# Result rows of a mixture of experts written by index past the empty slots, with another order of the last job, the eighth block's gates and the last block

## The chip, the cores and the metric

The kernel runs on one core of one Trainium2 chip, in float32. The metric is the device time of one execution, in microseconds (us). The program has five instruction streams: TensorE (PE in the rows, PEld for its weight loads), VectorE (DVE), ScalarE (ACT), GpSimd (POOL) and SyncE (SP). SP issues nearly all the loads, POOL the transfers by index. Sixteen DMA engines carry all transfers.

## The reference, cut to what matters

One encoder layer over 512 tokens of width 1024. The first part (a gated MLP group and a windowed attention group) gives `h`. Then comes the part that the change touches: 32 experts of width 256, of which each token uses two, and a gate of the embeddings `p`.

```python
def hier_moe(xt, ...):                 # top-1 of 4 groups, top-2 of its 8 experts
    ...
    for e in range(N_EXPERTS):
        hdn = jax.nn.silu(xt @ w_gate[e]) * (xt @ w_up[e])
        y = y + comb[:, e:e + 1] * (hdn @ w_down[e])
    return y

h = h + hier_moe(m, ...)
gate = jax.nn.sigmoid(h @ w_ple_gate[i] + b_ple_gate[i])
h = h + gate * rmsnorm(p[i] @ w_ple_proj[i], g_ple[i])
return rmsnorm(h, g_final)
```

## The kernel before, in words

**Front part, to about 200 us.** Projections, the gated MLP and the attention, with weights and inputs split into two parts of float32r (`mm3`), and the routing. Near 55 us the split of the queries ends (`V.tensor_tensor(qs...)`, the last operation on the way to the scores); near 82 us SP starts to load `w_out` (`s5a<-in_wo`, `s5c<-in_wo`), which ACT and DVE split (`load_parts`).

**Experts, about 190 to 471 us.** The two rows of each token (one per chosen expert) are sorted into slots. An expert among the first 20 places has 64 slots, a later one 32 (`LATE = 20`); a slot without a token holds an index beyond 511. `jobs` are 17 pairs of experts: ten with 2 x 64 slots, the others with 2 x 32, among them job 5 (`EXTRA`), which takes what overflows from places 7 and 8. Job `j` gathers its tokens from `h_dr` by index (`tokens_in`; an index beyond the bound moves nothing), transposes and scales them (`tokens_T`, `tokens_T2`), multiplies by the gate and up weights (`gate_up`), applies SiLU (`hidden`), transposes (`hidden_T`), multiplies by the down weights (`down`) and adds this to the scaled token rows (`base`, `scaled`) in one of two buffers `yo[j % 2]`. `rows_out(j)` then writes the whole buffer, empty slots too, to its rows of the DRAM tensor `y_dr` (1728 rows of 4 KB) with one plain DMA from POOL; jobs 15 and 16 stay on the chip. The weights of a pair of experts are 6 MB; SP loads them into seats as these come free, at most three loads in flight (`pace`).

**Blocks.** The 512 tokens are sorted by the job that ends their second row, and finished in nine blocks: 0 to 6 of 64 tokens, 7 and 8 of 32 (four column quarters side by side, `shape`, `chunk`). Block `b` gathers its tokens' two rows from `y_dr` (`f_in`, after job `FETCH[b]`), adds them (`f_add`), adds rows that have not gone through DRAM by a matmul with a 0/1 matrix (`f_sel`, `f_add2`), transposes (`f_T`, `f_T2`), multiplies by the 1024x1024 gate weights in eight steps `k` (`f_gate`), adds the bias, applies the sigmoid and the product with the `p` part (`f_post`), sums the squares (`total`), takes the root (`rstd`; for block 8 `ROOT` with ACT's square root) and writes out by index (`f_norm`, `f_out`).

**Order of the work.** `Plan` records every operation with its dependences, an estimated cost and a rank, and `issue` then sends them out greedily: the operation that could begin first by the estimate, then the lowest rank. So each engine's order is fixed when the program is built. `plan.gate` makes the recorded operations wait for others, `plan.behind` places them after others in the order, and `plan.fill` lets dummy matmuls into bank 7 (`filler`, line 361) fill gaps that the plan expects on TensorE. Nearly every instruction is recorded on line 238 or, for two or more matmuls issued together, line 169.

**The end.** In job 16 (the last) the order is: `f_sel`, `f_T` and `gate_up`, `hidden`, then `f_gate(7)` with all eight steps, `down`, `scaled` (the rows `own`), the fillers, the transposes of block 8 with `own`, `f_sel(8)`, `f_gate(8)`, its bias and sigmoid, and the last norm.

Of the kernel before, what the change touches and what calls it, by code (L numbers as in the profile page):

```python
# [4 lines left out]

# [31 lines left out]
WORK = (8, 9, 11, 12, 13, 14, 15)  # L37
SEL = (4, 12), (5, 13), (6, 14), (7, 15), (8, 15), (8, 16)
SETTLE = 5
P_AT = (6, 7, 8, 9, 10, 11, 12, 14)  # L40
SIZE = dict(a=2048, e=1024, b=2048, c=2048, d=1024, s1=6144,
            **{f"s{i}{h}": 2048 for i in (0, 2, 3, 4, 5, 6) for h in "acb"})
# [7 lines left out]
def f32(v):  # L50
    return v.bitcast(F32)
# [6 lines left out]
LOW7 = 0  # L58
# [27 lines left out]
class Plan:  # L86
# [45 lines left out]
    def note(self, e, method, call, args, kw):  # L132
        outs = [kw["out"] if "out" in kw else args[0]] + ([kw["accum_out"]] if "accum_out" in kw else [])
        ins = [getattr(a, "ap", a) if type(a) is bass.IndirectOffsetOnAxis else a
               for a in (*args[("out" not in kw):], *[v for k, v in kw.items() if k not in ("out", "accum_out")])]
        ins = [a for a in ins if isinstance(a, AP)]
        joins = e == "T" and bool(self.unit)
        i, after = self.unit[0] if joins else len(self.ops), set(self.gate)
        for a, writes in [(a, False) for a in ins] + [(a, True) for a in outs]:
            where = self.where(a)  # L140
            if where is None:
                continue
            place, box = where
            kept = []
            for j, b, w in self.mem.get(place, ()):
                hit = box[0] < b[1] and b[0] < box[1] and box[2] < b[3] and b[2] < box[3]

                if (hit and (w or writes) or b[4] != box[4]) and j != i:
                    after.add(j)
                covered = writes and box[0] <= b[0] and b[1] <= box[1] and box[2] <= b[2] and b[3] <= box[3]  # L150
                if not covered or j == i:
                    kept.append((j, b, w))
            self.mem[place] = kept + [(i, box, writes)]
            if e == "T" and writes:
                after.add(self.psum.get(place, i))
                self.psum[place] = i
        after.discard(i)
        first = outs[0]
        busy, late = self.cost(e, method, first, args, kw)
        size = 0  # L160
        if "dma_start" in method:
            first = next(a for a in (first, *ins) if a.space != bass.MemoryType.DRAM)
            size = 4 * first.free_size() * first.shape[0] / 360e3
        if joins:
            o = self.ops[i]
            first, last = (o[6], o[7], o[8]), (call, args, kw)
            o[1] += busy
            o[4] |= after
            o[6:10] = lambda: [c(*a, **k) for c, a, k in (first, last)], (), {}, (o[9] | self.behind) - o[4]  # L169
            return  # L170
        assert self.unit is None or e == "T"
        if self.unit is not None:
            self.unit.append(i)
        self.ops.append([e, busy, late, size, after, self.rank, call, args, kw, self.behind - after, self.fill, self.slack if e == "T" else 0.0])
# [82 lines left out]
def layer(ctx, tc, I, out):  # L257
# [5 lines left out]
    dr = ctx.enter_context(tc.tile_pool(name="dr", bufs=1, space=bass.MemoryType.DRAM))  # L263
    bank = [pp.tile([128, 512], F32, name=f"bank{i}") for i in range(8)]
    h_dr = dr.tile([512, 1024], F32, name="h_dr")
    y_dr = dr.tile([Y_ROWS, 1024], F32, name="y_dr")
    pace = dr.tile([128, 64], F32, name="pace")

    class Region:
# [44 lines left out]
    wr = pool.tile([128, 8, 36], F32, name="wr")  # L314
    tris = pool.tile([128, 128], BF, name="tris")
    oness = pool.tile([128, 128], BF, name="oness")
    small = pool.tile([128, 216], F32, name="small")
    gtmp = pool.tile([128, 512], F32, name="gtmp")
    idx = small[:, 0:17].bitcast(I32)
    fidx = small[:, 17:41].bitcast(I32)  # L320
    bad = small[:, 41:42].bitcast(I32)
    fst = small[:, 44:52]
# [33 lines left out]
        T.matmul(ps, lh, rl, start=False, stop=False)  # L356
        T.matmul(ps, ll, rh, start=False, stop=last)

    def filler(g):

        return lambda: nc.tensor.matmul(bank[g], oness, oness[:, None, :].to_broadcast([128, 4, 128]), start=True, stop=True)  # L361


    plan.on = True
# [108 lines left out]
    for g in range(4):  # L473
        q_ = q32[g % 2]
        V.scalar_tensor_tensor(q_, bank[g], 0.125, rbc, op0=OP.mult, op1=OP.mult)
        for v in range(2):
            p = slice(64 * v, 64 * v + 64)
            h = v * 4 + g
            S.activation(qs[h][p], q_[p], AF.Copy)
            V.tensor_tensor(qs[h][64 - 64 * v:128 - 64 * v], q_[p], f32(qs[h][p]), op=OP.subtract)  # L480


    f5, fe = Region("s5b"), Region("e")
# [470 lines left out]
    for p, o in sides:  # L954
        V.tensor_copy(WC[p, :, 0:3], bank[WB][p, 0:18].rearrange("p (a b c) -> p a b c", a=3, b=3, c=2)[:, :, :, o])


    plan.gate = set()
    by = [len(TILES[place[e]]) - 1 or 1 for e in range(FIRST)]
# [13 lines left out]
    def tables():  # L973
# [50 lines left out]
                    "p (a b c) -> p a b c", a=3, b=n // 2, c=2)[:, :, :, o])  # L1024

        take(256, n, slice(3, LATE // 2), sides)

        flat2 = lambda v: v.rearrange("p a b -> p (a b)")
        V.tensor_scalar(BX, P2, 6.5, None, op0=OP.is_gt)
# [12 lines left out]
        with plan.together():  # L1042
          for t in range(4):
            for i in range(2):
                T.matmul(bank[7][0:64, 320:320 + 4 * m], hq[:, 4 * i + t].rearrange("p a b -> p (a b)"),
                         RNQ[:, i, t].rearrange("p a b -> p (a b)"), start=t == 0 and i == 0, stop=t == 3 and i == 1)
        take(320, m, slice(LATE // 2, 17), ((slice(0, 32), 0), (slice(32, 64), 1)))
        V.tensor_copy(WC[64:128, :, LATE // 2:17], WC[0:64, :, LATE // 2:17])

        V.tensor_tensor(t3, P2[:, 0], P2[:, 1], op=OP.max)  # L1050
# [212 lines left out]

    def rows_out(j):
        r0, n = first_row(j), rows_of(j)[1].stop
        G.dma_start(y_dr[r0:r0 + n, :], yo[j % 2][:n])

    epsc = att_st[:, 28:29]

# [69 lines left out]
    def row(n, b):  # L1339
        return L[n + "q" if quarters(b) else n]  # L1340
# [4 lines left out]
    def f_in(b, n):  # L1345

        m = shape(b)[0]
        for i, v in enumerate((at("fy", b), at("fz", b))):
            G.memset(v, 0.0)
            ix = qidx[:, 2 * i + b - 5:2 * i + b - 4] if m == 4 else fidx[:, 8 * i + 8 + b:8 * i + 9 + b]  # L1350
            gather_rows(v, pieces(y_dr[0:n, :], m), ix, m * n - 1)

    def f_out(b):
        m = shape(b)[0]
# [41 lines left out]
    def rstd(b, i, g):  # L1396
        rsqrt(stat(b, i + 1), stat(b, 4), 1, -0.5 / 1024, stat(b, 5), bank[g][:, 500:501])
# [43 lines left out]
        S.activation(fT[:, 0:w // 2], bank[g][:, 0:w // 2], AF.Copy)  # L1441
        V.tensor_copy(fT[:, w // 2:w], bank[g][:, w // 2:w])

    def f_gate(b, g=3, cs=None):
        n, t, m = shape(b)
        cs = (0, m) if cs is None else cs
        for k in range(8):
            w = L["wg"][k // 2][:, k % 2]
            with plan.together():
                for q in range(n):  # L1450
                    T.matmul(bank[g][t * q:t * q + t, cs[0]:cs[1]], L["fT"][:, chunk(b, k)],
                             w[:, q * m + cs[0]:q * m + cs[1]], start=k == 0, stop=k == 7)

    def f_post(b, g=3, cs=None, o=2, root=False):
        c = slice(0, shape(b)[2]) if cs is None else slice(*cs)
        fx, fy, fple = at("fx", b)[:, c], at("fy", b)[:, c], at("fple", b)[:, c]
        V.tensor_tensor(fy, bank[g][:, c], row("bpl", b)[:, c], op=OP.add)
        S.activation(fy, fy, AF.Sigmoid)
        done = {len(plan.ops) - 1}
        V.tensor_tensor(fy, fy, fple, op=OP.mult)  # L1460
        V.tensor_tensor(fx, fx, fy, op=OP.add)
        if root and ROOT:

            plan.behind = done
            S.activation(stat(b, 7), epsc, AF.Sqrt)
            plan.behind = set()
            V.tensor_tensor_reduce(out=fy, in0=fx, in1=fx, scale=1.0, scalar=0.0, op0=OP.mult, op1=OP.add, accum_out=stat(b, o))
        else:
            S.activation(fy, fx, AF.Square, accum_out=stat(b, o))
# [9 lines left out]
    if True:  # L1479
# [15 lines left out]
        for j in range(nj):  # L1495
# [19 lines left out]
                plan.fill = filler(7) if j else None  # L1515
            load_after(j, 0)
            hidden(j)
            if norm is not None:
                plan.rank = R + LOW
                total(norm, 2, 7 if j < nj - 1 else 2)  # L1520
                plan.rank = R
# [19 lines left out]
                    f_add2(c, 4 if c > 6 else 3)  # L1541
            if j == nj - 1:
                plan.rank = R + LOW7
                f_gate(7)
                f_post(7)
                total(7, 2, 3)
                rstd(7, 2, 3)
                f_norm(7)
                f_out(7)
                plan.rank = R  # L1550
            if j + 1 < nj:
                base(j + 1)
# [9 lines left out]
            if b is not None:  # L1562
                f_T(b, FT[rows_of(j)[1].stop == 64])
                f_T2(b, FT[rows_of(j)[1].stop == 64])
            down(j, 1)
            scaled(j)
            if j < nj - 2:
                rows_out(j)
# [21 lines left out]
            for c in range(9):  # L1590
                if fetch[c] == j:
                    f_in(c, rows_n[c])

        fx, last = at("fx", 8), tokens_of(8, nj - 1)[:64]
        for i in range(2):
            T.matmul(bank[i][:, 0:128], fx[:, 128 * i:128 * i + 128], ident, start=True, stop=False, skip_group_check=True)
        for k in (0, 2, 1, 3, 4, 6, 5, 7):
            T.matmul(bank[k % 2][:, 32 * (k // 2):32 * (k // 2) + 32], own[:, 128 * k:128 * k + 128], last, start=False, stop=True,
                     skip_group_check=True)
        S.activation(L["fT"][:, 0:128], bank[0][:, 0:128], AF.Copy)  # L1600
        V.tensor_copy(L["fT"][:, 128:256], bank[1][:, 0:128])
        plan.rank += 1
        f_sel(8, [nj - 1], 4, src=own)
        f_add2(8, 4)
        plan.rank -= 1
        f_gate(8, 2)
        f_post(8, 2, root=True)
        total(8, 2, 3)
        if ROOT:
# [185 lines left out]
```

## Time and profile before

| what | value |
|---|---|
| median of 3 runs | 491.39 us (488.01, 491.39, 494.56) |
| the profiled execution: time, span of its trace | 489.91 us, 488.1 us |
| busy share of the span: PE, DVE, ACT, POOL | 95%, 62%, 35%, 20% |
| granted TensorE clock, mean | 0.984 |
| moved by DMA | 144.72 MB |

The span is the stretch that the trace covers; 1.81 us of the profiled execution lie outside it. Busy shares are means over stages with different limits. A clock of 1.00 means TensorE's full 2.4 GHz, 0.5 the lower level of 1.2 GHz. In a row of instructions the bracket says how long the engine sat idle before it and what ended that wait.

### The profile page before, as it was taken

How to read it: one execution, taken by the hardware profiler on the slowest of the kernel's cores; microseconds unless marked ns; L12 is line 12 of the kernel's file. 1: busy time of each engine (PE TensorE's matmuls, PEld its weight loads, DVE VectorE, ACT ScalarE, POOL GpSimd, SP SyncE). 2: the span in 40 equal slices, each digit the busy share in tenths (PEclk: the TensorE clock that was granted, in tenths of full speed). 3: DMA queues.
4: the chain of work that ended last, by engine and by line, in shares of the span. 5: the costliest groups of instructions: out<-in, count | busy, mean ns of one | idle time of the engine just before them, and what ended most of it. 6: DMA issues, size and time to landing. Idle time of an engine off the chain costs nothing.

```text
span 488.1 us, 8538 instructions
## 1 busy us (share of the span) xinstructions
PE 462.8 (95%) x2973; PEld 259.4 (53%) x2973; DVE 305.0 (62%) x991; ACT 172.7 (35%) x354; POOL 100.0 (20%) x131
## 2 busy tenths in 40 slices
PE   7999999999999998999999999799999898798994
PEld 4888887868678896543334333233343333333352
DVE  4985998899853566894435344426466665565553
ACT  4958576899913340100001001013212223213131
POOL 0000112313210002011541223312143233123001
PEclk9999999999999999999999999999999899799999
DMA  8874101356779986999988999999999999999801
GB/s 282 268 263 149 54 0 43 131 173 228 278 297 426 361 296 214 353 385 419 412 314 278 399 418 419 415 368 400 381 342 430 396 392 370 387 383 378 307 4 48
DMA packets 26590, 144.72 MB, mean 296 GB/s; under 512 B 4200, under 2 KB 4748, under 8 KB 14638
## 3 DMA queue, kind: packets, MB, share of 16 engines
q1 hardware_dynamic: 20190, 124.61, 67.3%
q0 software_dynamic: 6352, 19.51, 10.7%
q8 instruction: 25, 0.41, 0.3%
q14 instruction: 23, 0.19, 0.1%
HBM read 136.37 MB, written 10.77 MB: 301 GB/s over the span
## 4 chain that ended last, share of the span: by engine, by line
PE 82%; DMA 7%; DVE 6%; issue 2%; ACT 2%; SPq 0%; POOL 0%; POOLq 0%; ACTq 0%; DVEq 0%
PE bank L169 48%; PE bank L238 33%; DMA y_dr<-b 4%; DMA s3c<-y_dr,small 2%; DMA b<-in_xwq 1%; DVE b L238 1%; PE bank L361 1%; DVE c L238 1%; DVE s3a L238 1%; DVE small L238 1%; DVE s2c L238 1%; DVE e L238 0%; DVE s3c L238 0%; DVE s L238 0%; SPq L238 0%
## 5 line engine op out<-in xcount | busy, mean ns | idle before, releaser
L238 DVE TENSOR_SCALAR small<-small 128x1 f32<-128x1 f32 (+4 forms) x207 | 45.9, 223 | 4.3
L169 PE MATMUL bank<-s,c 128*32 128x256 f32 (+1 forms) x176 | 48.5, 491 | 0.0
L238 ACT ACTIVATE e<-bank,small 128x256 f32<-128x256 f32 (+1 forms) x17 | 8.0, 471 | 103.6 <-PE bank L169 103.6
L238 DVE SCALAR_TENSOR_TENSOR b<-bank,small,b 128x512 f32<-128x512 f32 (+1 forms) x32 | 24.0, 749 | 23.5 <-PE bank L169 23.3
L238 ACT ACT_TABLE_LOAD x20 | 25.7, 1283 | 9.8 <-PE bank L169 4.5
L238 DVE TENSOR_TENSOR c<-bank,cst 128x512 f32<-128x512 f32 (+1 forms) x34 | 18.6, 573 | 16.1 <-PE bank L169 15.4
L238 ACT ACTIVATE s3c<-s3c 128x512 f32<-128x512 f32 (+1 forms) x9 | 5.2, 582 | 64.7 <-DVE s3c L238 64.7
L238 ACT ACTIVATE s<-s,small 128x256 f32<-128x256 f32 (+1 forms) x48 | 25.5, 556 | 3.6 <-DVE small L238 3.6
L169 PE MATMUL bank<-s,e 128*64 128x512 f32 (+1 forms) x64 | 26.2, 626 | 0.0
L169 PE MATMUL bank<-s4b,e 128*64 128x512 f32 (+1 forms) x56 | 22.5, 630 | 2.7 <-DVE small L238 2.7
L238 POOL DMA_INDIRECT a<-h_dr,small x17 | 17.1, 1004 | 38.8 <-issue 12.0
L238 DVE SCALAR_TENSOR_TENSOR e<-bank,small,e 128x256 f32<-128x256 f32 (+1 forms) x17 | 8.2, 485 | 26.0 <-ACT e L238 24.4
L169 PE MATMUL bank<-s0a,c 128*32 128x256 f32 (+1 forms) x96 | 22.9, 454 | 0.4 <-DVE c L238 0.4
L169 PE MATMUL bank<-s5a,c 128*32 128x256 f32 (+1 forms) x96 | 22.9, 454 | 0.0
L238 DVE TENSOR_SCALAR b<-a,small 64x512 f32<-64x512 f32 (+2 forms) x23 | 14.4, 625 | 12.9 <-DMA y_dr<-b 9.9
L169 PE MATMUL bank<-s5b,e 128*64 128x512 f32 (+1 forms) x64 | 22.3, 597 | 0.0
L169 PE MATMUL bank<-s0b,e 128*64 128x512 f32 (+1 forms) x64 | 22.3, 596 | 0.0
L169 PE MATMUL bank<-s5c,c 128*32 128x256 f32 (+1 forms) x96 | 22.1, 451 | 0.0
L169 PE MATMUL bank<-s0c,c 128*32 128x256 f32 (+1 forms) x96 | 22.1, 451 | 0.0
L169 PE MATMUL bank<-s4a,c 128*32 128x256 f32 (+1 forms) x80 | 21.9, 498 | 0.0
L169 PE MATMUL bank<-s2a,s6c 128*64 128x512 f32 (+1 forms) x88 | 17.7, 560 | 4.1 <-ACT s6c L238 2.5
L238 POOL DMA_INDIRECT s3c<-y_dr,small x14 | 15.3, 1090 | 28.2 <-DMA y_dr<-b 25.7
(428 smaller groups left out, 1218.9 us busy)
## 6 DMA issues: line engine op xcount, KB each, us to landing
s<-in_wgu SPq DMA_DIRECT2D x7, 2048.0 KB
s0a<-in_wgu SPq DMA_DIRECT2D x7, 1024.0 KB
s0c<-in_wgu SPq DMA_DIRECT2D x7, 1024.0 KB
s0b<-in_wdn SPq DMA_DIRECT2D x7, 1024.0 KB
s5a<-in_wgu SPq DMA_DIRECT2D x7, 1024.0 KB
s<-in_wdn SPq DMA_DIRECT2D x7, 1024.0 KB
s5c<-in_wgu SPq DMA_DIRECT2D x7, 1024.0 KB
s4a<-in_wgu SPq DMA_DIRECT2D x7, 1024.0 KB
```

Source lines behind the costliest of these rows:

```text
L169: o[6:10] = lambda: [c(*a, **k) for c, a, k in (first, last)], (), {}, (o[9] | self.behind) - o[4]
L238: call(*args, **kw)
L361: return lambda: nc.tensor.matmul(bank[g], oness, oness[:, None, :].to_broadcast([128, 4, 128]), start=True, stop=True)
```

## The change

1. `y_dr` is a plain DRAM tensor with 17 views that are declared disjoint, one per job. Near the front part's 55 us, SP fills its 1728 rows from `x` with four DMAs from DRAM to DRAM, so that every row holds finite numbers.
2. `rows_for` computes on DVE a table `yidx` of destination rows, with 4096 added for an empty slot. `rows_out` writes by that index with a bound, so empty slots are passed over. The writes are declared independent of the gathers already recorded in `fetched`.
3. In the last job, only steps 0 to 4 of `f_gate(7)` stand ahead of `down`; steps 5 to 7 and the rest of block 7 (`f_post` to `f_out`) come behind it. ACT's sigmoid table is loaded by a dummy activation right after the SiLU.
4. For block 8, a matmul with the identity puts the bias into bank 2 ahead of the gates, four gate steps come before `f_sel(8)` and four after it, the sigmoid reads the bank directly, and at most nine fillers stand ahead of the last sum.

```diff
+AHEAD = 5
...
-    y_dr = dr.tile([Y_ROWS, 1024], F32, name="y_dr")
+    y_dr = nc.dram_tensor("y_dr", (Y_ROWS, 1024), F32).ap()
+
+    y_of = bass_types.dram_disjoint_views(y_dr, 17)
+    fetched = []
...
+    yidx = small[:, 216:233].bitcast(I32)
...
+    def filler(g, most=99):
+
+        left = [most]
+
+        def fill():
+            if left[0]:
+                left[0] -= 1
+                nc.tensor.matmul(bank[g], oness, oness[:, None, :].to_broadcast([128, 4, 128]), start=True, stop=True)
+
+        return fill
...
+    plan.gate = {len(plan.ops) - 1}
+    for i in range(0, Y_ROWS, 512):
+        n = min(512, Y_ROWS - i)
+        Y.dma_start(y_dr[i:i + n, :], I["x"][0:n, :])
+    plan.gate = set()
...
+    def rows_for(p, a, b, n, r0):
+
+        y = yidx[p, a:b]
+        V.tensor_scalar(y, idx[p, a:b], 511.5, 4096.0, op0=OP.is_gt, op1=OP.mult)
+        if b > a + 1:
+            V.scalar_tensor_tensor(y, iota32[p, 0:b - a], float(n), y, op0=OP.mult, op1=OP.add)
+        V.tensor_scalar(y, y, tokp1[p, 0:1], r0 - 1.0, op0=OP.add, op1=OP.add)
...
+    rows_for(slice(0, 128), 0, 3, 128, 64)
...
+        rows_for(slice(0, 128), 3, LATE // 2, 128, 64 + 384)
...
+        rows_for(slice(0, 64), LATE // 2, 16, 64, 64 + 64 * LATE)
+        rows_for(slice(0, 64), 16, 17, 64, 0)
...
-        G.dma_start(y_dr[r0:r0 + n, :], yo[j % 2][:n])
+        c = 16 if j == EXTRA else jobs[j][0] // 2
+        ix = bass.IndirectOffsetOnAxis(ap=yidx[:n, c:c + 1], axis=0)
+        plan.note("G", "indirect_dma_start", put, (), dict(out=y_dr[r0:r0 + n, :], out_offset=ix, in_=yo[j % 2][:n], in_offset=None,
+                                                           bounds_check=r0 + n - 1, oob_is_err=False, view=y_of[c]))
+
+    def put(out, view, **kw):
+
+        w = nc.gpsimd.indirect_dma_start(out=view, **kw)
+        for f in fetched:
+            tc.declare_no_dep(w.ins, f.ins, reason="other rows")
...
-    def f_gate(b, g=3, cs=None):
+    def f_gate(b, g=3, cs=None, ks=range(8), first=True):
...
-        V.tensor_tensor(fy, bank[g][:, c], row("bpl", b)[:, c], op=OP.add)
-        S.activation(fy, fy, AF.Sigmoid)
+        if root:
+
+            S.activation(fy, bank[g][:, c], AF.Sigmoid)
+        else:
+            V.tensor_tensor(fy, bank[g][:, c], row("bpl", b)[:, c], op=OP.add)
+            S.activation(fy, fy, AF.Sigmoid)
...
+            if j == nj - 1:
+
+                plan.behind = {len(plan.ops) - 2}
+                S.activation(stat(7, 7), epsc, AF.Sigmoid)
+                plan.behind = set()
...
-                f_gate(7)
-                f_post(7)
-                total(7, 2, 3)
-                rstd(7, 2, 3)
-                f_norm(7)
-                f_out(7)
+                f_gate(7, ks=range(AHEAD))
...
+        plan.behind = {plan.down}
+        plan.rank = R + LOW7
+        f_gate(7, ks=range(AHEAD, 8))
+        plan.behind = set()
+        f_post(7)
+        total(7, 2, 3)
+        rstd(7, 2, 3)
+        f_norm(7)
+        f_out(7)
...
+        plan.behind = {len(plan.ops) - 1}
+        with plan.together():
+            for q in range(4):
+                p = slice(32 * q, 32 * q + 32)
+                T.matmul(bank[2][p, 0:256], ident[:, p], row("bpl", 8), start=True, stop=False)
+        plan.behind = set()
...
-        plan.rank += 1
+        f_gate(8, 2, ks=range(4), first=False)
+        plan.behind = {len(plan.ops) - 1}
         f_sel(8, [nj - 1], 4, src=own)
+        plan.behind = set()
         f_add2(8, 4)
-        plan.rank -= 1
-        f_gate(8, 2)
+        f_gate(8, 2, ks=range(4, 8))
+        plan.fill = filler(7, 9)
```

## Rows read from the trace of the kernel before

**Rows 1.** Windows: busy us by engine (PE, PEld, DVE, ACT, POOL), granted clock, DMA share, GB/s.

```profile
300.00:320.00 20.00, 16.55 (x83) 6.65 (x84) 7.99 (x20) 2.27 (x6) 6.58 (x7) 0.91 1.01 409
400.00:420.00 20.00, 17.00 (x143) 6.32 (x142) 11.00 (x26) 5.40 (x8) 6.05 (x8) 1.00 0.99 383
```

**Rows 2.** Chain of waits that ended last: start us, us, what.

```profile
301.26 9.96 DMA y_dr<-b
...
395.90 8.46 DMA y_dr<-b
...
406.49 10.07 DMA s3c<-y_dr,small
```

**Rows 3.** Timeline around both stretches: who waited, and what ended the wait.

```profile
314.09 1.46 POOL L238 DMA_INDIRECT s3c<-y_dr,small  x1 [2.21 <-DMA y_dr<-b]
...
313.91 0.75 DVE L238 TENSOR_SCALAR b<-a,small 128x1024 f32<-128x1024 f32 x1 [2.70 <-issue]
...
315.05 1.00 PE L169 MATMUL bank<-s4b,e 128*64 128x512 f32 x1 [2.74 <-DVE small L238]
...
421.72 0.38 PE L169 MATMUL bank<-small,s3b 128*64 128x1 f32 x4 [1.87 <-ACT s3c L238]
```

**Rows 4.** Timeline: when job 14's seat s4a has landed, when TensorE uses it.

```profile
409.22 0.28 SPq L238 DMA_DIRECT2D pace<-s4a  x1
...
425.80 0.63 PE L169 MATMUL bank<-s4a,c 128*32 128x256 f32 x1
```

**Rows 5.** DMA: POOL's queue (packets, MB); issues, KB each, median us to landing.

```profile
q0 software_dynamic: 6352, 19.51, 10.7%
...
y_dr<-b POOLq DMA_DIRECT2D x10, 512.0 KB, 9.5
...
y_dr<-b POOLq DMA_DIRECT2D x5, 256.0 KB, 8.9
...
out<-s3c,small POOLq DMA_INDIRECT x9, 7.7
```

**Rows 6.** Tile y_dr: POOL's instructions, ns minimum, median, maximum.

```profile
L238 POOL DMA_DIRECT2D y_dr<-b x15: 567/597/730, 208.8 to 439.9; - x15
L238 POOL DMA_INDIRECT s3a<-y_dr,small x4: 998/1005/1020, 299.0 to 430.1; - x4
```

**Rows 7.** Windows of the front part and of full-rate loading, columns as before.

```profile
56.00:60.00 4.00, 4.00 (x22) 3.32 (x21) 3.97 (x15) 0.69 (x1) 0.62 (x1) 1.00 0.00 0
...
150.00:160.00 10.00, 10.00 (x60) 8.55 (x59) 4.13 (x18) 4.75 (x10) 0.17 (x1) 1.00 1.01 428
```

**Rows 8.** Timeline of the front part: end of query split, load, and its waiter.

```profile
54.92 0.69 DVE L238 TENSOR_TENSOR s0c<-s,s0c 64x512 fp32r<-64x512 f32 x1
...
82.53 0.80 SPq L238 DMA_DIRECT2D s5a<-in_wo  x2
...
86.44 0.73 ACT L238 ACTIVATE s4a<-s5a,cst 128x512 fp32r<-128x512 f32 x1 [3.87 <-DMA s5a<-in_wo]
```

**Rows 9.** Timeline: a small operation on slot tables.

```profile
210.24 0.16 DVE L238 TENSOR_SCALAR small<-bank 32x7 int32<-32x7 f32 x1
```

**Rows 10.** Timeline of the end: down, fillers, gates of block 8, its last sum.

```profile
469.14 0.59 PE L169 MATMUL bank<-s4b,e 128*32 128x512 f32 x1
...
471.19 0.82 PE L361 MATMUL bank<-oness 128*128 128x512 bf16 x3
...
477.31 1.05 PE L169 MATMUL bank<-s6b,s6c 128*32 128x256 f32 x16
478.29 3.19 PE L361 MATMUL bank<-oness 128*128 128x512 bf16 x14
478.42 0.42 DVE L238 TENSOR_TENSOR s3c<-bank,s3b 128x256 f32<-128x256 f32 x1 [1.02 <-PE bank L169]
...
480.60 0.08 DVE L238 DVE_READ_ACCUMULATOR2_ANT small<- 128x1 f32 x1
...
481.41 0.24 PE L169 MATMUL bank<-small,c 128*32 128x1 f32 x8
```

More of the change, by code (lines that the diff above doesn't have):

```diff
@@ L6 @@
 import concourse.bass as bass
+from concourse import bass_types
 import concourse.tile as tile
@@ L161, in note @@
         if "dma_start" in method:
-            first = next(a for a in (first, *ins) if a.space != bass.MemoryType.DRAM)
+            first = next((a for a in (first, *ins) if a.space != bass.MemoryType.DRAM), first)
             size = 4 * first.free_size() * first.shape[0] / 360e3
@@ L316, in layer @@
     oness = pool.tile([128, 128], BF, name="oness")
-    small = pool.tile([128, 216], F32, name="small")
+    small = pool.tile([128, 233], F32, name="small")
     gtmp = pool.tile([128, 512], F32, name="gtmp")
     idx = small[:, 0:17].bitcast(I32)
+    yidx = small[:, 216:233].bitcast(I32)
     fidx = small[:, 17:41].bitcast(I32)
@@ L357, in mm3 @@
         T.matmul(ps, ll, rh, start=False, stop=last)
-    def filler(g):
-        return lambda: nc.tensor.matmul(bank[g], oness, oness[:, None, :].to_broadcast([128, 4, 128]), start=True, stop=True)
+    def filler(g, most=99):
[5 more added lines that the diff above has]
+        return fill
     plan.on = True
@@ L955, in layer @@
         V.tensor_copy(WC[p, :, 0:3], bank[WB][p, 0:18].rearrange("p (a b c) -> p a b c", a=3, b=3, c=2)[:, :, :, o])
+    def rows_for(p, a, b, n, r0):
[4 more added lines that the diff above has]
+        V.tensor_scalar(y, y, tokp1[p, 0:1], r0 - 1.0, op0=OP.add, op1=OP.add)
+    plan.rank += 8
+    rows_for(slice(0, 128), 0, 3, 128, 64)
+    plan.rank -= 8
     plan.gate = set()
@@ L1351, in f_in, with kept @@
             gather_rows(v, pieces(y_dr[0:n, :], m), ix, m * n - 1)
+            if plan.on:
+                plan.ops[-1][6] = kept(plan.ops[-1][6])
+    def kept(call):
+        return lambda *args, **kw: fetched.append(call(*args, **kw))
     def f_out(b):
@@ L1442, in f_T2 @@
         V.tensor_copy(fT[:, w // 2:w], bank[g][:, w // 2:w])
-    def f_gate(b, g=3, cs=None):
+    def f_gate(b, g=3, cs=None, ks=range(8), first=True):
         n, t, m = shape(b)
         cs = (0, m) if cs is None else cs
-        for k in range(8):
+        for k in ks:
             w = L["wg"][k // 2][:, k % 2]
@@ L1451, in f_gate @@
                     T.matmul(bank[g][t * q:t * q + t, cs[0]:cs[1]], L["fT"][:, chunk(b, k)],
-                             w[:, q * m + cs[0]:q * m + cs[1]], start=k == 0, stop=k == 7)
+                             w[:, q * m + cs[0]:q * m + cs[1]], start=first and k == 0, stop=k == 7)
     def f_post(b, g=3, cs=None, o=2, root=False):
@@ L1565, in layer @@
             down(j, 1)
+            plan.down = len(plan.ops) - 1
             scaled(j)
@@ L1592, in layer @@
                     f_in(c, rows_n[c])
+        plan.behind = {plan.down}
[7 more added lines that the diff above has]
+        f_out(7)
+        plan.rank = R
         fx, last = at("fx", 8), tokens_of(8, nj - 1)[:64]
```

## Prediction

> **What bounds the kernel now.** I read the windows first. TensorE is busy 95% of the span; in the stage of the experts most windows of 20 us show it busy for 18 to 20 us, and the two worst are those of [rows 1], where it does 16.55 and 17.00 of 20. The DMA engines are full there too (1.01 and 0.99), so the second question is which of the two leads. [Rows 4] answer it: the load of s4a for job 14 has landed by 409.22, when SP's paced transfer behind it could go, and TensorE first reads it at 425.80. Weights are some 16 us ahead there; bytes alone do not hold TensorE up. What does hold it up stands in the chain of waits: between long runs of matmuls it goes through three transfers of `y_dr` [rows 2]. Around 301 us job 7's write is issued; DVE's `base` of job 9 must wait for it (it refills the same `yo`), and POOL's gather of block 1 too, so both begin only at about 314; TensorE, which needs a DVE copy queued behind that `base`, has sat idle 2.74 us by 315.05 [rows 3]. Its next matmuls then run long: 1.00 us in place of the 0.59 us that the same shape takes at [rows 10], first row, and the window's granted clock is 0.91. Around 396 us job 12's write takes 8.46 us, block 5's gather behind it 10.07 us, and TensorE waits 1.87 us for an activation fed by that sum [rows 2, 3]. So what a `y_dr` write is worth is read from these two holes. The third place is the end: after the last gates nothing overlaps, and each step removed is a step gained [rows 10].
>
> **The change part by part.** The sum is made against the profiled execution (489.91 us, of which 488.1 are span). That execution is 1.48 us below the median of the three runs, 491.39.
>
> *Smaller writes.* POOL's queue moved 19.51 MB [rows 5]. Of this the `y_dr` writes are 10 x 512 KB and 5 x 256 KB, 6.55 MB. Two loads of 1 MB, the 512 output rows of 4 KB and the 512 rows of `p` of 1 KB are 4.72 MB by the code. The remaining 8.24 MB must be the token gathers (1024 rows, 4.19 MB) and the gathers from `y_dr`: 4.05 MB, some 989 filled rows of 1600 written. The change therefore saves about 2.5 MB. At the 383 to 409 GB/s of [rows 1] that is 6 us of DMA time, but since the weights are ahead of TensorE I count none of it as such.
>
> What counts is when a write lands. Plain writes take 9.5 us at 512 KB and 8.9 at 256 KB, and output writes by index, also 256 KB, 7.7 [rows 5]. Size matters little, then: 0.6 us for half the bytes. If the small jobs were full, the ten large ones would hold 669 of 1280 rows, about 268 KB each, so a large write should land 0.6 us earlier by its size and up to 1.8 earlier by the row of output writes. A small write keeps most of its rows and gains 0 to 1.2. Against this, an instruction by index holds POOL 1.0 us in place of 0.6 [rows 6]; 0.4 us times 15 lies beside other work, except in front of a gather that has waited for this very write. The write also reads `yidx`, computed by DVE before its job's matmuls, so it adds no later wait. What is late next, if a write lands sooner, is the gather (10.07 us) or the matmul before the copy. I take 1.1 us in the first hole and 0.4 in the second: -1.5. Bounds: 0, and both holes gone with their slow clock, 2.74 + 1.87 us of waiting plus about 2.8 us of matmuls at half speed behind them, -7.4. The 2.8 is an estimate: eight matmuls, in pairs, 0.41 us too long in the first hole make 1.6 (1.00 against 0.59), and I add 1.2 for the second, where a matmul of the 256-column shape shows 0.63 [rows 4].
>
> *The fill.* 1728 rows of 4 KB are 7.08 MB, read and written in DRAM. SP may issue it when the last query split ends, 54.92 + 0.69 = 55.61 us [rows 8]. The DMA engines are idle from then (0.00 in [rows 7]) until `w_out` is loaded at 82.53; on SP nothing else is queued between, so no other issue waits. The cover is 26.9 us long, and it suffices from 263 GB/s up. No row shows a transfer from DRAM to DRAM. The nearest is loading at full rate, 428 GB/s [rows 7]: done by 72.2, cost 0. If each byte costs the engines twice, once in and once out, the rate is 214 GB/s and the end 88.7; `w_out`, first in line for ACT, which already waits 3.87 us for it [rows 8], would come up to 6.2 us later. ACT and then TensorE would shift by perhaps 4 of these, as ACT has little idle time behind that point. The bounds are 0 and +4; a gain is excluded, since nothing is removed. Neither row is near enough to decide, so I take +1.5.
>
> *Tables.* `rows_for` adds 11 small DVE operations by the four calls. At 0.16 us [rows 9] that is 1.8 us of DVE if none overlapped, in a stretch where TensorE does nearly 20 of 20 us. I take +0.3, bounds 0 and +1.8.
>
> *The last job.* Three steps of `f_gate(7)` move from before `down` to behind it. There the rows now show 0.82 us of fillers (471.19), while ACT and DVE scale `own` [rows 10]. A step of block 7 is half of a 16-record row, at most 0.53 us; three cover the scaling. TensorE's real work is the same, the fillers go: -0.8, if `hidden_T`'s copy is ready early enough for `down` to move up from 469.14; otherwise fillers return in front of it and the gain is 0. `f_post(7)` to `f_out(7)` come later by about 2 us; DVE and ACT have room for them while block 8's gates run, and their output write is issued before block 8's. If that cover failed, one DVE operation of 0.42 us would stand in block 8's way.
>
> *Block 8.* The bias matmul costs TensorE one more step, +0.5, partly in a wait for the copies of `fT`. DVE's bias addition goes: 0.42 us and a handover of 0.04 [rows 10], -0.46. The 14 fillers from 478.29 end after 481.4, while the sum of squares that the next matmul needs is read out at 480.68; nine fillers take 9/14 x 3.19 = 2.05 us and no longer delay it: -0.7. The table load moved up hides behind the matmuls. Together -0.7, and with the last job -1.5; bounds +0.5 and -2.
>
> **The sum.** -1.5 (writes) + 1.5 (fill) + 0.3 (tables) - 1.5 (end) = -1.2 us: 488.7 for an execution like the profiled one, 490.2 at the median. A measurement of this kernel can tell about 2% from no change, some 10 us. I forecast 490, no change that can be told.
>
> **The rivals.** *The fill collides.* At 214 GB/s the sum becomes -1.5 + 4 + 0.3 - 1.5 = +1.3, 492.7 at the median; it decides from 263 GB/s down, and grows by the full delay below that: at 180 GB/s the fill ends at 94.9, 12 us past the load, and the kernel is some 7 us slower (499). For it: reading and writing share the same engines and memory. Against it: the engines have an empty stretch, and their share measures how full they are, not how often a byte passes. The Trainium skill, "DMA: Bandwidth & Descriptors", section "Latency and other measured facts", lists copies between HBM tensors at 207 to 214 GB/s per direction, even at a good pitch; by it, as an estimate, the fill ends near 90 us and this rival holds. No run here shows such a copy yet.
>
> *The writes land early enough.* Both holes close and the clock stays up: -7.4 + 0.5 + 0.3 - 1.5 = -8.1, 483.3, with a little more if other waits for writes go too (DVE and POOL each wait for more of them). For it: in both holes the wait ends exactly with the write. Against it: landing depends little on size.
>
> *Passing over slots shortens nothing.* A transfer is over when its fullest engine is; empty slots stand together at the end of each 64, so some engines may simply go idle. Then 0 + 1.5 + 0.3 - 1.5 + up to 0.4 per write in the chain: +1.1, 492.5.
>
> **How the numbers follow.** Forecast 0.45; the fill collides 0.25, of which 0.08 at the low rates that cost over 2%; writes early enough 0.18, of which half with more than 2%; nothing shortened 0.12. That makes faster by over 2% 0.10, within 2% 0.82, slower 0.08. The range holds 8 in 10: from 482, the case of the early writes with a little more, to 497, between a collision at 214 and one at 180 GB/s.
>
> **What would show it.** The fill: DMA share between 56 and 92 us, and whether ACT's wait at s5a<-in_wo grows beyond 3.87 us. The writes: their landing, DVE's `base` and the gathers behind job 7 and job 12, and TensorE's busy time and clock in the windows of [rows 1]. The end: fillers gone behind `down`, and from the end of block 8's gates to its last sum some 2 us in place of 3. I am wrong if the order that the plan gives out changes elsewhere, since new operations shift every later choice, or if a gather now waits for more writes than it needs.

## The result: slower by 1.2%, and the profile after

The changed kernel takes 496.91 us (median of 6 runs, 494.11 to 501.07) where the kernel before, on the same chip, takes 490.94 (488.01 to 494.56). The ratio is 1.0124, 95% interval 1.0085 to 1.0162: 6.1 us more, 4.2 to 8.0. The forecast was 1.2 us less. Ratios here and below are made on one chip and leave disturbed runs out, so they are not always the quotient of two medians. The profiled execution after has a span of 495.2 us.

I look for the loss in the windows first. Here are windows of the kernel after (us; busy time of PE, PEld, DVE, ACT, POOL; clock, DMA share, GB/s):

```profile
300.00:320.00 20.00, 18.79 (x104) 7.16 (x101) 10.10 (x28) 3.22 (x7) 7.02 (x7) 1.00 0.99 393
320.00:340.00 20.00, 15.73 (x81) 5.49 (x77) 6.28 (x11) 3.51 (x6) 4.93 (x5) 0.99 1.00 388
340.00:360.00 20.00, 20.00 (x86) 6.98 (x88) 9.56 (x27) 2.99 (x5) 4.58 (x5) 0.84 1.00 370
...
400.00:420.00 20.00, 18.77 (x152) 7.15 (x156) 13.07 (x37) 5.08 (x8) 7.48 (x10) 0.91 1.01 403
```

At these times the holes of [rows 1] have filled up: 16.55 became 18.79 and 17.00 became 18.77. (The work there comes 8 to 12 us later than before: job 7's write is issued at 308.98 and no longer at 301.26, job 12's at 408.38 and no longer at 395.90.) But a new hole stands between 320 and 340, with a lower granted clock after it. What VectorE waits for, and what TensorE waits for from it, tells more (us in total, times, longest us). First before, then after:

```profile
DVE b L238 <- DMA y_dr<-b: 9.9, 7, 3.3
...
PE bank L169 <- DVE e L238: 0.3, 1, 0.3
```

```profile
DVE b L240 <- DMA y_dr<-b,small: 32.8, 11, 6.3
...
PE bank L171 <- DVE e L240: 9.0, 9, 3.8
```

`base`, the scaling that refills `yo`, now waits three times as long for the result writes, and TensorE waits 9.0 us in place of 0.3 for `e`, the tile of `hidden` and `hidden_T`. The timeline of after shows what this does at one of the 11 places (start us, us, instruction, idle time before it):

```profile
334.20 0.69 DVE L240 TENSOR_TENSOR s3a<-s3a,s3c 128x512 f32<-128x512 f32 x1
338.80 0.75 DVE L240 TENSOR_SCALAR b<-a,small 128x1024 f32<-128x1024 f32 x1 [3.91 <-DMA y_dr<-b,small]
339.47 0.48 DVE L240 SCALAR_TENSOR_TENSOR e<-bank,small,e 128x256 f32<-128x256 f32 x1
...
340.00 0.69 PE L171 MATMUL bank<-cst,e 128*128 128x128 f32 x2 [3.77 <-DVE e L240]
...
344.73 1.06 PE L171 MATMUL bank<-s0b,e 128*64 128x512 f32 x1
```

VectorE runs its instructions in the order of the plan. It stands 3.91 us at `base`, and the product of `hidden`, queued behind it, begins only when `base` is done. TensorE needs that product for `hidden_T` and idles 3.77 us, and a `down` matmul a little later takes 1.06 us in place of 0.59; the clock of the window from 340 to 360 is 0.84. The same step before:

```profile
332.07 0.74 DVE L238 TENSOR_SCALAR b<-a,small 128x1024 f32<-128x1024 f32 x1
...
335.51 0.47 DVE L238 SCALAR_TENSOR_TENSOR e<-bank,small,e 128x256 f32<-128x256 f32 x1
...
336.04 0.44 PE L169 MATMUL bank<-cst,e 128*128 128x128 f32 x2 [0.88 <-DVE small L238]
...
338.17 0.59 PE L169 MATMUL bank<-s0b,e 128*64 128x512 f32 x1
```

There the wait for the write is over when VectorE comes to `base`. The chain of waits after has the same picture once more, at job 11's write:

```profile
388.82 9.98 DMA y_dr<-b,small
398.82 0.48 DVE b L240
399.33 0.50 DVE e L240
399.88 6.68 PE bank L171 x30
```

Are the writes themselves slow? POOL's instructions of `y_dr` after (ns minimum/median/maximum), then landing of all transfers of `y_dr`, then the queue and the medians to landing:

```profile
L1307 POOL DMA_INDIRECT y_dr<-b,small x15: 935/1022/1527, 210.3 to 442.0; - x15
...
DMA to landing us min/median/max: 3.4/8.1/12.6
```

```profile
q0 software_dynamic: 6352, 17.00, 9.4%
...
y_dr<-b,small POOLq DMA_INDIRECT x15, 9.1
```

The queue moves 2.51 MB less than in [rows 5], as worked out. A write lands in 9.1 us, where 9.5 and 8.9 stood. So little was gained by passing over slots, but nothing that explains 6 us was lost either.

**Where the new order comes from.** `Plan` gives every DMA a transfer time from the bytes of the first operand that isn't in DRAM:

```python
first = next((a for a in (first, *ins) if a.space != bass.MemoryType.DRAM), first)
size = 4 * first.free_size() * first.shape[0] / 360e3
```

For the plain write that operand is `yo`: 1.46 us for 512 KB, 0.73 for 256 KB. For the write by index the change lists `out_offset` ahead of `in_`, so the first operand outside DRAM is the column of 128 offsets: 0.5 KB, 0.0014 us. The plan now holds the write for done 1.46 us sooner, finds that `base` can begin sooner, and sends it out ahead of work that TensorE needs. That is theory 1. The rivals: the writes themselves (theory 2); the new end; the fill and the tables.

### The profile page after: what moved, and what is told of

Read it like the earlier page. It is cut to its first block, busy times and chain, and to the rows that moved or that the text cites. A ratio compares the mean times of both kernels' runs of the same rounds, so it can differ in the third digit from the quotient of the medians.

```text
span 495.2 us, 8565 instructions
## 1 busy us (share of the span) xinstructions
PE 465.5 (94%) x2973; PEld 259.4 (52%) x2973; DVE 304.0 (61%) x1001; ACT 173.1 (35%) x355; POOL 106.9 (22%) x131
## 5 line engine op out<-in xcount | busy, mean ns | idle before, releaser
L240 DVE TENSOR_SCALAR small<-small 128x1 f32<-128x1 f32 (+5 forms) x211 | 46.3, 222 | 4.2
L171 PE MATMUL bank<-s,c 128*32 128x256 f32 (+1 forms) x176 | 47.2, 479 | 0.0
L240 DVE TENSOR_SCALAR b<-a,small 64x512 f32<-64x512 f32 (+2 forms) x23 | 14.0, 610 | 33.2 <-DMA y_dr<-b,small 32.8
L171 PE MATMUL bank<-s0b,e 128*64 128x512 f32 (+1 forms) x64 | 24.6, 662 | 0.2 <-DVE e L240 0.2
L171 PE MATMUL bank<-s5b,e 128*64 128x512 f32 (+1 forms) x64 | 24.7, 663 | 0.0
L171 PE MATMUL bank<-s,e 128*64 128x512 f32 (+1 forms) x64 | 24.5, 598 | 0.0
L1307 POOL DMA_INDIRECT y_dr<-b,small x15 | 15.5, 1037 | 40.8 <-DVE b L240 18.0
L171 PE MATMUL bank<-s0c,c 128*32 128x256 f32 (+1 forms) x96 | 23.7, 469 | 0.0
L171 PE MATMUL bank<-s5c,c 128*32 128x256 f32 (+1 forms) x96 | 23.7, 469 | 0.0
L171 PE MATMUL bank<-s6a,s3b 128*64 128x512 f32 (+1 forms) x88 | 20.6, 645 | 1.9 <-DVE s3b L240 1.6
L171 PE MATMUL bank<-s4b,e 128*64 128x512 f32 (+1 forms) x56 | 20.9, 598 | 1.0 <-DVE e L240 1.0
```

What stands on the lines that cost most here:

```text
L240: call(*args, **kw)
L1307: w = nc.gpsimd.indirect_dma_start(out=view, **kw)
```

## The experiments

**Mend the size, and break it in the kernel before.** `e1_size` changes only the order of two names:

```diff
-dict(out=y_dr[r0:r0 + n, :], out_offset=ix, in_=yo[j % 2][:n], in_offset=None,
+dict(out=y_dr[r0:r0 + n, :], in_=yo[j % 2][:n], out_offset=ix, in_offset=None,
```

> The changed kernel with one thing mended: the planner counts an indirect write with the bytes of yo (512 or 256 KB, 1.46 or 0.73 us of transfer) and no longer with those of its column of offsets (0.5 KB, 0.0014 us). Theory 1 (the planner took the indirect writes for nearly free, put the scaling that waits for them ahead of other work in VectorE's order, and VectorE stood still behind it): most of the 6.0 us come back, 490 to 492 us, VectorE's waits for y_dr writes fall from 32.8 us in 11 places to about 10 us. Theory 2 (the indirect writes themselves land too late, or hold GpSimd up): the order changes and the time stays, 495 to 497 us.

Measured: 491.21 us beside 494.67 for before, ratio 0.9868 (0.9797 to 0.9939). `e2_before_wrong` is the kernel before with one more line in `rows_out`:

```diff
 G.dma_start(y_dr[r0:r0 + n, :], yo[j % 2][:n])
+plan.ops[-1][3] = 4 * n / 360e3
```

> The kernel before with its direct writes, and only the planner's size of them made wrong in the same way (0.5 KB for 256 or 512 KB). Nothing else differs. Theory 1: as slow as the changed kernel, 495 to 498 us, with VectorE waiting some 30 us for y_dr writes. Theory 2: no change, 490 to 491.5 us.

Measured: 506.61 us, ratio 1.0255 (1.0185 to 1.0324). VectorE's waits, first of e1_size, then of e2_before_wrong:

```profile
DVE b L240 <- DMA y_dr<-b,small: 8.7, 5, 2.7
```

```profile
DVE b L238 <- DMA y_dr<-b: 34.6, 11, 6.7
```

Both ends hold: with writes by index and the right size the waits are as short as before and the kernel is faster than before; with plain writes and the wrong size they are as long as after, and it is slower, by more than theory 1 said (12.5 us, not 4 to 7). Theory 2 falls. (e4_writes below, with the same size in the plan, shows 8.8 us in 5 places.) These two also rule out that the end, the fill or the tables cost the 6 us, since e1_size has them all.

**The end alone, and the writes alone.** `e3_tail` is before with items 3 and 4 of the change, `e4_writes` before with items 1 and 2 and the size mended.

> The kernel before with the new order of the end alone (block 7's gates in two parts, the sigmoid table loaded early, block 8's bias on TensorE and its gates in two halves, nine filler matmuls): writes, fill and tables as before. The prediction's term: 1.5 us less, 489.4 us (bounds 0.5 more and 2 less). By the trace after, where the stretch from the last job's silu to the last output takes 17.84 us in place of 18.05: 0.2 us less, 490.7 us. Rival (the new order costs part of the 6 us): 492 us or more.

> The kernel before with the fill, the row tables and the indirect writes, their size mended for the planner, and the old order of the end. Theory 1: 490 to 492 us; beside the first of these runs it gives the worth of the end. By the prediction's own terms it is 491.2 us (fill 1.5 more, tables 0.3 more, writes 1.5 less). Theory 2 (the writes themselves): 495 to 497 us.

Measured: e3_tail 0.9946 (0.9900 to 0.9993), 2.7 us less, 0.3 to 4.9; e4_writes 1.0016 (0.9973 to 1.0059), 0.8 us more, from 1.3 less to 2.9 more. The end in the traces, from the last job's SiLU on ACT to the last output's issue on POOL, before and then e3_tail:

```profile
465.54 0.47 ACT L238 ACTIVATE e<-bank,small 64x256 f32<-64x256 f32 x1 [0.71 <-PE bank L169]
...
483.59 0.96 POOL L238 DMA_INDIRECT out<-s3c,small  x1 [4.05 <-DVE s3c L238]
```

```profile
469.53 0.47 ACT L239 ACTIVATE e<-bank,small 64x256 f32<-64x256 f32 x1 [0.71 <-PE bank L170]
...
482.33 2.12 PE L367 MATMUL bank<-oness 128*128 128x512 bf16 x9
...
486.55 0.97 POOL L239 DMA_INDIRECT out<-s3c,small  x1 [2.90 <-DVE s3c L239]
```

18.05 us became 17.02: 1.03 less. The new end helps, and e1_size has the same 17.02; in the changed kernel itself the stretch takes 17.84, so there most of this gain is lost.

**Is it the wait, or the other order by itself?** `e6_no_writes` is the changed kernel with the body of `put` replaced by `pass`, `e7_size_no_writes` is the same done to e1_size.

> The changed kernel with its orders of VectorE, TensorE, ScalarE and SyncE untouched, the planner's wrong size included, but the 15 result writes not issued: the gathers read the rows of the fill, so the expert results are left out of the output. Theory 1 (the wait behind the write is what costs): VectorE no longer stands at the scaling, 7 to 11 us less than the changed kernel, 0.975 to 0.990 of the kernel before. Rival (the other order costs by itself, wait or no wait): within 2 us of the changed kernel, 1.008 to 1.016 of before.

> The control to e6_no_writes: the changed kernel with the size mended, and the 15 result writes not issued (the expert results are left out of the output in the same way). Theory 1: it gains little on e1_size, 0 to 3 us, since its waits for the writes are 8.7 us and mostly covered, and it ends within 2 us of e6_no_writes. Rival of e6_no_writes: it stays 4 us or more below e6_no_writes.

Measured: 481.74 us, ratio 0.9827 (0.9768 to 0.9886), and 482.87 us, 0.9877 (0.9828 to 0.9927). Two windows of after, and the same two of e6_no_writes, which has the same order on TensorE, VectorE, ScalarE and SyncE:

```profile
200.00:300.00 100.00, 97.19 (x568) 38.59 (x565) 51.12 (x184) 7.15 (x16) 25.89 (x33) 1.00 0.92 352
300.00:400.00 100.00, 89.69 (x556) 33.92 (x551) 47.27 (x121) 19.20 (x34) 28.52 (x30) 0.95 1.00 387
```

```profile
200.00:300.00 100.00, 98.95 (x577) 39.16 (x575) 54.48 (x208) 7.54 (x16) 19.96 (x29) 1.00 0.91 352
300.00:400.00 100.00, 98.20 (x676) 38.14 (x672) 55.74 (x142) 23.85 (x41) 28.28 (x32) 1.00 1.01 391
```

Without the writes the order costs nothing: TensorE is busy 10.3 us more in these 200 us, and its clock stays at 1.00 in both. By the ratios, from two sets of runs, e6_no_writes is 14.6 us faster than the changed kernel, more than the 7 to 11 expected. The two kernels without writes end 1.1 us apart by their medians and 2.5 us by their ratios, the one with the wrong size ahead, though with the writes their ratios are 1.0124 and 0.9868. (Leaving writes out also takes their bytes away and frees the gathers; e7_size_no_writes, at the ratio of e1_size within the intervals, bounds what that is worth.)

**Which of the consumers?** The size enters the plan in three ways: when `base` may begin, when the gathers may, and how long the plan's DMA line is taken. `e9_base_mended` leaves the size wrong and gives the time back to `base` alone; `e10_base_wrong` has the right size and takes it from `base` alone:

```diff
+lag += self.more.get((best, ops[i][0]), 0.0)
...
+plan.more[len(plan.ops) - 1, "V"] = n * 4096 / 360e3
```

(This is e9; e10 has the same lines on e1_size, with a minus ahead of `n`.)

> The changed kernel with the planner's wrong size left as it is, but one edge mended: for the scaling on VectorE (and for nothing else) the write is planned to land 1.46 or 0.73 us later, as with the right size. Theory 1a (it is the planned landing that the scaling sees): as e1_size, 0.983 to 0.995 of the kernel before, VectorE's waits for y_dr writes near 10 us. Theory 1b (it is the rest: the transfer time that the plan's DMA line lacks, and the earlier gathers): as the changed kernel, 1.006 to 1.018, waits near 30 us.

> The other half: the changed kernel with the size mended for the DMA line and the gathers, and only the scaling on VectorE planned with the write landing 1.46 or 0.73 us sooner, as with the wrong size. Theory 1a: as the changed kernel, 1.006 to 1.018 of the kernel before. Theory 1b: as e1_size, 0.983 to 0.995.

Measured: e9_base_mended 486.96 us, 0.9880 (0.9801 to 0.9960); e10_base_wrong 503.03 us, 1.0212 (1.0132 to 1.0291). First e9, then e10:

```profile
DVE b L242 <- DMA y_dr<-b,small: 16.8, 6, 4.6
```

```profile
DVE b L242 <- DMA y_dr<-b,small: 25.6, 9, 4.9
```

It is the planned landing that `base` sees: theory 1a, with the opposite result from the opposite edit (e10_base_wrong lies a little above its range). No effect of the rest shows within the intervals. One part of the expectation failed: e9's waits are 16.8 us, not near 10, and it is as fast as e1_size. The sum of VectorE's waits is no price. TensorE's own idle time comes nearer: between 200 and 460 us it is 13.1 us before, 17.1 after, 20.7 in e2_before_wrong, 10.7 in e9_base_mended and 21.1 in e10_base_wrong. Where it idles depends on the whole order: in e10_base_wrong it waits longest for the blocks' tiles and not for `e`, once 3.53 us behind `base` again (VectorE stands 4.39 us there) and once 5.89 us behind a block's sum that waits for its gather. Its two largest waits:

```profile
PE bank L172 <- DVE s3a L242: 6.3, 2, 5.9
PE bank L172 <- DVE s3b L242: 6.0, 3, 3.5
```

**Would the true landing be better still?** `e5_late` (on e1_size) and `e8_before_late` (on before) tell the plan that a result write lands 8.6 us after its issue, the median of all transfers of `y_dr` in the traces before and of e1_size, in place of 4.6 (in the plan 1.04 us on POOL, 1.1 up to the transfer, 1.46 for 512 KB, 1.0 to the landing). The gathers' own landing stays as the plan had it, 3.9 us by the same sum with 0.73 for 256 KB, where the trace before has medians of 7.0 and 8.3.

> The changed kernel with the planner's size mended as in e1_size, and told besides that a result write lands 5.0 us after its transfer in place of 1.0, 8.6 us from issue in all, as the traces show it. Theory 1 (what counts is how far the planner's landing lies from the real one): the scaling moves still later in VectorE's order, its waits for y_dr writes fall from 8.7 us to under 3 us, and the time falls 0 to 3 us below e1_size, to 0.980 to 0.990 of the kernel before. Rival: the waits that are left were covered, and the later scaling shifts other work to its harm: 0 to 3 us more than e1_size.

> The kernel before with its direct writes, and only the planner told that a result write lands 5.0 us after its transfer in place of 1.0. Theory 1: its 9.9 us of waits of VectorE for y_dr writes fall below 3 us, 0 to 3 us less than before, 0.994 to 1.000. Rival: the scaling was placed well and later work suffers: 1.000 to 1.006.

Measured: e5_late 502.21 us, 1.0257 (1.0205 to 1.0309); e8_before_late 500.94 us, 1.0232 (1.0190 to 1.0275). The waits at `base` are gone in both, as expected, and both kernels are slower by more than after is. Neither the gain nor the size of the rival's loss was foreseen: theory 1 in the form "the closer to the true landing, the faster" falls. In e5_late TensorE's longest waits are for the tokens of the next jobs, whose gather from `h_dr` stands on POOL behind a block's gather that waits for job 7's write (POOL's two gathers, then TensorE's waits in total):

```profile
312.18 1.04 POOL L1400 DMA_INDIRECT s3c<-y_dr,small  x1 [6.89 <-DMA y_dr<-b,small]
...
314.84 1.00 POOL L240 DMA_INDIRECT a<-h_dr,small  x1 [0.30 <-issue]
...
PE bank L171 <- DMA a<-h_dr,small: 10.9, 3, 7.6
```

So I took e5_late apart: the late landing for `base` alone, and for the gathers alone.

> e5_late (2.6% slower than before) taken apart: the size mended, and only the scaling on VectorE planned 4.0 us later behind its write; the gathers as in e1_size. Theory 2a (the scaling planned late falls behind work that comes with the next job's silu and sums, and the job's own output then waits for it): 1.015 to 1.03 of before. Theory 2b (the late gathers cost, they move the last blocks): 0.985 to 0.997.

> The other half of e5_late: only the gathers on GpSimd planned 4.0 us later behind the writes, the scaling as in e1_size. Theory 2a: 0.985 to 0.997 of the kernel before. Theory 2b: 1.015 to 1.03.

Measured: e11_base_late 488.05 us, 0.9919 (0.9874 to 0.9964); e12_gather_late 510.32 us, 1.0325 (1.0224 to 1.0426). Theory 2b holds: the late gathers cost, e12_gather_late a little more than its range said. One place stands out in it; POOL first, then VectorE, then TensorE:

```profile
302.94 1.02 POOL L1311 DMA_INDIRECT y_dr<-b,small  x1 [0.32 <-DVE b L242]
312.51 1.47 POOL L1403 DMA_INDIRECT s3c<-y_dr,small  x1 [8.56 <-DMA y_dr<-b,small]
314.29 1.01 POOL L1403 DMA_INDIRECT s3a<-y_dr,small  x1 [0.31 <-issue]
...
322.32 0.69 DVE L242 TENSOR_TENSOR s3a<-s3c,s3a 128x512 f32<-128x512 f32 x1 [8.96 <-issue]
322.93 0.42 DVE L242 COPY e<-bank 128x256 f32<-128x256 f32 x1
...
323.40 1.11 PE L172 MATMUL bank<-s4b,e 128*64 128x512 f32 x1 [8.96 <-DVE small L242]
```

The first block's gather came out behind job 7's write and waited for it. VectorE stood 8.96 us at the block's sum of the two gathered tiles, ahead of the copy of `hidden_T`, and TensorE idled as long. (The row names no releaser; the second of the two gathers was issued at 314.29.) In the kernel before the first gather of this kind began at 297.5, ahead of job 7's write at 301.26 [rows 2]:

```profile
L238 POOL DMA_INDIRECT s3c<-y_dr,small x14: 998/1045/1456, 297.5 to 450.5; - x14
```

It is the same mechanism as in the changed kernel, with another operation at which VectorE stands. Why the plan, told of a later gather, still put the sum ahead of the copy stays open; that it takes the gather to land sooner than it does would fit, but no run tried it.

## Why the prediction was wrong, point by point

**The bound.** Right: TensorE's holes come from VectorE standing behind transfers of `y_dr`, with matmuls at the lower clock after them. That was read from [rows 3] as a wait that the writes might shorten. It should also have been read as an order: how much a write costs depends on where the plan puts the operation that waits for it.

**The step that failed** is the one that the sum doesn't hold. Every term was priced in the order of the kernel before; "the order that the plan gives out changes elsewhere" stands in the last part, put down to new operations that shift later choices, without a price. Its term for the writes, -1.5 with 0 as the worst, let the wait at `base` only fall; it rose from 9.9 to 32.8 us. What changed the order was the rewritten write's own estimate, 0.0014 us for 1.46, readable in the kernel: its `note` lists the offsets first, and `Plan` takes the first operand outside DRAM. The runs price it: the changed kernel's ratio less that of e1_size is 2.6%, 12.6 us, and the ends of the two intervals, from two sets of runs, put it between 7 and 18; on one chip e10_base_wrong less e9_base_mended, for the edge to `base` alone, is 3.3% of 490 us, 16 us.

**Smaller writes, fill, tables.** Predicted -1.5 + 1.5 + 0.3 = +0.3; e4_writes has +0.8, from -1.3 to +2.9. The sum holds, its terms less so. By the traces the fill is free. It began at 42.29, not 55.6 (`plan.gate` fixed its place in SP's order; nothing held it until the last query split, which begins at 54.56), and was over before `w_out` came. SyncE's issues and ScalarE's wait for `w_out`, after, and then two of the windows of the fill:

```profile
42.29 2.63 SPq L240 DMA_DIRECT2D y_dr<-in_x  x4
82.14 0.80 SPq L240 DMA_DIRECT2D s5a<-in_wo  x2
...
86.09 0.72 ACT L240 ACTIVATE s4a<-s5a,cst 128x512 fp32r<-128x512 f32 x1 [3.90 <-DMA s5a<-in_wo]
```

```profile
58.00:62.00 4.00, 4.00 (x22) 3.39 (x21) 4.00 (x17) 2.09 (x6) 0.26 (x1) 1.00 0.88 295
62.00:66.00 4.00, 4.00 (x21) 3.42 (x20) 3.96 (x16) 2.23 (x8) 0.93 (x2) 1.00 1.01 319
...
70.00:75.00 5.00, 5.00 (x24) 4.25 (x24) 5.00 (x22) 2.25 (x8) 1.15 (x2) 1.00 0.00 0
```

ScalarE waits 3.90 us for `w_out` where [rows 8] have 3.87, and the DMA engines stand idle again from 70. The rival of the fill's collision falls. The copy runs at 295 and 319 GB/s. The Trainium skill, "DMA: Bandwidth & Descriptors", section "Latency and other measured facts", has 207 to 214 GB/s, by which it would have collided, for copies of tiles of 128 rows of 16 KiB at the better row pitches. For these contiguous rows of 4 KB the trace does not agree, and the measurement decides. The tables were not measured apart.

For the writes the rival "passing over slots shortens nothing" came nearest: 9.1 us to landing beside 9.5 and 8.9 in [rows 5]. Over all traces with the writes, the medians are 7.9 to 9.3 us by index, and for plain writes 8.5 to 9.5 at 512 KB and 6.7 to 8.9 at 256 KB. So the 0.6 us that the prediction read for half the bytes is that of one trace; the other three have 1.5 to 2.5. In e4_writes TensorE's wait in the first hole is 1.97 us in place of 2.74 and the 1.87 us of the second are still there: about half of the -1.5, which the ratio cannot resolve. The rival in which the writes land early enough takes +0.5 for the fill where the forecast takes +1.5, and gives no reason.

**The end.** Predicted -1.5, bounds +0.5 to -2. e3_tail measures -2.7, -0.3 to -4.9, and its trace shows -1.03 for the stretch itself. The mechanism behind the fillers is right: nine of them take 2.12 us where 2.05 was said. The rest of the gain outside the stretch isn't explained; the interval reaches down to 0.3.

**Together.** Without the mis-sized estimate the change is what e1_size shows: 0.9868, 6.5 us less than before, 3 to 10. It beats both kernels. That is more than e3_tail and e4_writes add up to (-1.9 us), though the intervals meet. Whether the parts help each other or the plan merely came out luckily stays open; three orders with the same edits (e1_size, e9_base_mended, e11_base_late) lie at 0.987, 0.988 and 0.992.

## What to carry to other kernels

When the order of instructions comes out of a program's own estimates, read every operation that a change rewrites as an input to them too: print the estimate before and after, and compare the orders of the engines before pricing anything. An operation that waits for a transfer is not costly by its wait but by what is queued behind it on its engine: look at the next instruction there that the bounding engine needs. And one estimate brought nearer to the truth, beside others that are not, need not give a better order, so run an edit of the estimates as any other edit.

## What the runs showed of the hardware

Writes by index that pass over empty rows, 2.51 of 6.55 MB in all, land hardly sooner than the full plain ones, 9.1 us against 9.5 and 8.9 (medians of 7.9 to 9.3 against 8.5 to 9.5 and 6.7 to 8.9 over all traces), with the DMA engines 92 to 100% busy between 200 and 400 us. A copy from DRAM to DRAM in four DMAs ran at 295 to 319 GB/s beside matmuls without a mark on them: TensorE was busy 4.00 of 4 us in each of those windows, at a clock of 1.00.
